# A decoder layer on one core: the last 1024 columns of the first MLP product by seven products, and the rotary queries placed elsewhere

## The chip, the cores and the metric

The kernel runs on one core of one Trainium2 chip. The metric is the time of one execution on the device in microseconds (us), smaller is better. TensorE (PE in the profile) multiplies matrices; its weight loads are shown apart as PEld. VectorE (DVE), ScalarE (ACT) and GpSimd (POOL) do the work between the products, and SyncE (SP) issues most of the DMAs. POOL and ACT issue some DMAs as well.

## The reference, cut to what matters

The program is one layer of a hybrid decoder for 512 tokens of width 1024, all in float32. Two token mixers (gated linear attention, GLA, and multi-head latent attention, MLA) work on the same normalised input, are merged by gates and projected; then comes an MLP of width 4096. Each half ends in a layer norm over a scaled residual.

```python
def reference(x, ...):
    cos, sin = rope_tables(positions)
    h = layer_norm(x, ln_in_g, ln_in_b)
    mix = token_mixer(h, cos, sin, w_in, ...)
    h = layer_norm(DEEPNORM_ALPHA * h + mix, ln1_g, ln1_b)
    ff = jnp.square(jax.nn.relu(h @ w_ff1)) @ w_ff2
    return layer_norm(DEEPNORM_ALPHA * h + ff, ln2_g, ln2_b)
```

Within the token mixer, `h @ w_in` gives, among others, 2048 columns of gate logits (1024 for each branch) and the latent queries. The queries of the eight MLA heads come out of the normalised latent queries by `w_q_b`, 128 columns a head without and 64 with a rotary embedding. In the MLP, h is 512 x 1024 and w_ff1 is 1024 x 4096.

## The kernel before, in words

**Numbers.** Each float32 operand of a product is split into a high part `hi` of a reduced format (float32r) and the remainder `lo`. A product of one block is three matmuls: hi x hi, hi x lo, lo x hi (L238 to L240 where weights are the stationary side, L271 to L273 where tokens are). Splitting a weight tile is an ACT copy (L185) and a DVE subtraction (L186).

**Weights.** All weight tiles form one list, `stream`, in the order of their use. `plan` appends entries, and `pump(i)` (L162) sees to it that entries up to i + 2 are loaded (SP DMA into `wraw`, L173) and those up to i + 1 are split (two further for entries marked `res` or `ahead`). A tile is 128 x 1024 floats. There are three buffers for `wraw` and two each for `whi` and `wlo`; a new split can start when the last matmul that read the older of the two tiles is done. Further tiles share three rings of buffers: A with 24 (`wq`, `hraw`, `hx`, `sh1`, `hid0`, `latT`, `gt`, `xh`, `xl` and others), B with 22 of half the size, and C with 8. An entry may also have a `src`, a tile that other instructions make, and a `post`, work that is done when it has been split.

**Order.** The program is written in one order, with generators (`spawn`, `tick`) that slip the side work of DVE, ACT and POOL between the matmuls. A scheduler then sets the order of the instructions on each engine before the run, by priority in the written order and by what is ready, and assigns the buffers.

**Stages around the change.** In order: input norm (`ln_transpose`, L399; it writes the transposed, normalised h, and for later also its unsplit values to DRAM as `hrawd`, L420); latents, q, k, v, r projections with GLA between them; first half of the gates (`gemm_fm`); second half of the gates by the seven-product unit (`gemm_unit("g1", ...)`, L997); `y_gla(0)`; `mla_qr(0)` (rotary queries of heads 0 to 3, L802); head pair 0; `y_gla(1)`; `mla_qr(1)`; pairs 1 to 3; output projection; norm (`h1T`, the transposed result in eight pairs of B tiles); then the MLP in four slices of 1024 hidden columns (`ci` 0 to 3). In each slice the first product with relu and square makes eight blocks of 128 hidden columns (`hid`), and the second product adds them up. Slices 0 to 2 use seven products in the second product (`win_f2`, L1257, fourteen steps `n` in the list WIN). Slice 3 uses plain products in both.

**The seven-product scheme.** A product of 2 x 2 blocks is made from seven block products instead of eight, after sums of operand blocks. In the unit the left side is four blocks of the weights, the right side four blocks of h: token halves (256 columns) by even and odd inner blocks. The list FMO (L307) gives the seven: 11, 21, t1, 22, t2, t3, t4. 11, 21, 22 are loaded blocks, t1 to t4 sums of blocks. `u_load` (L990) loads t1 and t3 as one block by SP and adds a second by an accumulating POOL DMA (L995); t2 and t4 come from t1 by DVE additions (`u_sum`, L324), as `post` of 22 and of t2. The sums of h are made by `op_sums` (L964): four sums on DVE for each of four pairs of blocks, then a split; it reads the unsplit h back from DRAM (L970). After each product partial sums are copied and added (`e1`, `e5`, `u2`, L1028 to L1041) and a quarter of the result is handed to `evac`, which for the gates is a tanh (L1054). A tile of the unit holds two inner blocks and four feature blocks, two tiles for each product; its matmuls (L1021 to L1023) have 256 columns.

**The slice to be replaced.** Slice 3 makes eight blocks in two passes of four, each 96 matmuls of 512 columns. ACT makes relu and its square as `hid0` (L1301, L1315), POOL squares again in full precision (L1316), DVE takes the remainder (L1317). The second product of the slice (`f2last`) then works through tokens 0 to 255 first, then 256 to 383, then the rest.

**Rotary queries.** `mla_qr(g)` multiplies the latent queries `qlT` (three inner blocks, two weight tiles of 512 and 256 values a lane) into 36 matmuls of 256 columns, rotates the result on DVE (L487 to L489), splits it (L114, L115) and transposes it (L821) into `QS`, which the heads read. `qlT` and the latent keys `ckT` wait in DRAM since the latents stage; `after` (L1072) loads the five tiles back (L1080).

Of the kernel before, what the change touches and what calls it, by code (L numbers as in the profile page):

```python
# [19 lines left out]
P = 128  # L20
# [32 lines left out]
def tile_hybrid_block(ctx: ExitStack, tc: tile.TileContext, I, out, dbg=None):  # L53
# [254 lines left out]
    UNITS = {"g1": ("w_in", C_G + D)}  # L308
# [13 lines left out]
    def u_sum(key, a, to, hf, x):  # L322
        t = WQ[key, (to, hf)] = WQ[key, (a, hf)]
        vtt(t, t, x, op=ALU.add)  # L324


    for key in UNITS:
        PL[key] = []
        for op, _ in FMO:
            for hf in range(2):  # L330
                PL[key].append(len(stream))
                e = {"nk": 2, "n": T, "res": False}
                if op[0] != "t":
                    e["dmas"] = [(slice(0, 2), u_src(key, int(op[0]) - 1, int(op[1]) - 1, hf), None)]
                else:
                    e["src"] = lambda q=(key, (op, hf)): WQ[q]
                if op == "22":
                    e["post"] = lambda raw, q=(key, "t1", "t2", hf): u_sum(*q, raw)
                elif op == "t2":
                    e["post"] = lambda raw, q=(key, "t2", "t4", hf): u_sum(*q, WQ[key, ("21", q[3])])  # L340
                stream.append(e)
    PL["yg", 0] = plan("w_o_gla", 0, T)
    plan_qr(0)
# [6 lines left out]
    plan_pair(0)  # L350
    PL["yg", 1] = plan("w_o_gla", T, T)
    plan_qr(1)
# [17 lines left out]
    F1 = [((0, 4), (4, 2), (6, 2))] + [tuple((b, 2) for b in range(0, 8, 2))] * 2 + [((0, 4), (4, 4))]  # L370
# [28 lines left out]
    def ln_transpose(rows, g, b, outs, hf, alt=False, n="h0"):  # L399
        tk = slice(hf * 256, (hf + 1) * 256)  # L400
        for k in range(NK):
            if len(outs) <= k:
                outs.append(A([P, 2, T], F32R, n) if n == "h0" else (B([P, T], F32R, n), B([P, T], F32R, n)))
            p = MM() if alt and k in (4, 5) else PX()
            for i in range(2):
                nc.tensor.transpose(p[:, i * P:(i + 1) * P], rows[2 * hf + i][:, k * P:(k + 1) * P], ident)
            tmp = B([P, 256], F32, "lnt")
            hi, lo = part(outs[k], 0, tk), part(outs[k], 1, tk)
            ha = act(hi, p[:, :256], AF.Identity, scale=g[:, k:k + 1], bias=b[:, k:k + 1])
            if alt and k % 2:  # L410
                act(tmp, p[:, :256], AF.Identity, scale=g[:, k:k + 1], bias=b[:, k:k + 1])
            else:
                vts(tmp, p[:, :256], g[:, k:k + 1], b[:, k:k + 1], op0=ALU.mult, op1=ALU.add)
# [10 lines left out]
    hT, rawd = [], []  # L424
# [539 lines left out]
    def op_sums(srcs, rest, new, ops):  # L964
        raws = []
# [24 lines left out]
    def u_load(key, op):  # L990
        for hf in range(2):
            t = WQ[key, (op, hf)] = A([P, 2, T], F32, "wq")
            nc.sync.dma_start(t, u_src(key, *{"21": (1, 0)}.get(op, (0, 1)), hf))
            if op != "21":
                nc.gpsimd.dma_start(t, u_src(key, *{"t1": (0, 0), "t3": (1, 1)}[op], hf), accum_op=ALU.add)  # L995

    def gemm_unit(key, ops, evac, after=None):  # L997

        bank, e1, e5, u2 = {}, {}, {}, {}
        nk = 2  # L1000
        for n, (op, ph) in enumerate(FMO):
            items = PL[key][2 * n:2 * n + 2]
            for g in range(2):
                bk = ("a" if ph in (0, 3, 6, 4) else "b", g)
                opens = ph in (0, 2, 1)
                if opens:
                    bank[bk] = (PX if ph == 1 else MM)()
                o = bank[bk]
                for hf, it in enumerate(items):
                    pump(it)  # L1010
                    hi, lo = stream[it]["w"]
                    for pp in range(nk):
                        while len(ops) <= nk * hf + pp:
                            tick(3)
                        xh, xl = ops[nk * hf + pp][ph]
                        for a in range(2):
                            c = slice((2 * g + a) * P, (2 * g + a + 1) * P)
                            oa = o[:, a * 256:(a + 1) * 256]
                            first = opens and hf == 0 and pp == 0 and a == 0
                            last = hf == 4 // nk - 1 and pp == nk - 1  # L1020
                            mm(oa, hi[:, pp, c], xh, start=first, stop=False, skip_group_check=True)  # L1021
                            mm(oa, hi[:, pp, c], xl, start=False, stop=False, skip_group_check=True)  # L1022
                            mm(oa, lo[:, pp, c], xh, start=False, stop=last, skip_group_check=True)  # L1023
                        if pp % 2:
                            tick(3)
# [3 lines left out]
                elif ph == 1:  # L1029
                    vtt(e1[g], o, e1[g], op=ALU.add)  # L1030
                    evac(0, 0, g, e1[g], None)
# [3 lines left out]
                elif ph == 3:  # L1035
# [3 lines left out]
                    evac(1, 0, g, u2[g], None)  # L1039
                elif ph == 6:  # L1040
                    vtt(e5[g], e5[g], o, op=ALU.subtract)  # L1041
                    evac(1, 1, g, e5[g], None)
                elif ph == 4:
                    evac(0, 1, g, o, None)
            if after:
                after(op)

# [14 lines left out]
    def h_sums():  # L1062
        yield from op_sums(hT, rawd,
# [8 lines left out]
    def after(op):  # L1072
# [3 lines left out]
        if op == "t4":  # L1076
            for outs, rest in ((qlT, qld), (ckT, ckd)):
# [179 lines left out]
    def win_f2(ci, hid):  # L1257
        bank = {}
        for n, (op, hf, ph) in enumerate(WIN):
# [28 lines left out]
            if n == 9 and ci + 1 < FC - 1:  # L1288
                win_load(ci + 1)

    WT = {}
    for ci in range(FC):
# [6 lines left out]
        def ev_h(a, ps):  # L1299
            r = B([P, T], F32, "relu")  # L1300
            act(r, ps, AF.Relu)  # L1301
            if win:
                if a % 2 == 0:
                    hid.append({"R": A([P, 2, T], F32, "hr")})
                ops = hid[-1]
                R = ops["R"]
                act(R[:, a % 2, :], r, AF.Square)
                if a % 2:
                    h1 = A([P, 2, 2, 256], F32R, "h1p")
                    split(R[:, :, :256], h1[:, 0], h1[:, 1])  # L1310
                    ops[0], ops[1] = [(h1[:, 0, i], h1[:, 1, i]) for i in range(2)]
                    spawn(win_hid(R, ops))
                return
            hh = A([P, 2, T], F32R, "hid0")
            act(hh[:, 0, :], r, AF.Square)  # L1315
            gtt(r, r, r, op=ALU.mult)  # L1316
            vtt(hh[:, 1, :], r, f(hh[:, 0, :]), op=ALU.subtract)  # L1317
            hid.append(hh)
# [15 lines left out]
        else:  # L1334
            bg, bb = bcast_row("ln2_g"), bcast_row("ln2_b")
            gemm_tm(PL["f2last"], hid, T, ev_res, tts=(0, 1))
# [67 lines left out]
```

## Time and profile before

| | us |
|---|---|
| runs before (3): median, lowest, highest | 903.59, 901.25, 905.59 |
| the profiled execution: its time | 902.01 |
| its span in the trace | 900.2 |
| first matmul of the gates' unit to the first of y_gla(0) | 275.21 to 317.31 |
| mla_qr(0), first to last matmul | 339.09 to 343.29 |
| last step list of win_f2 (slice 2) | 767.0 to 804.9 |
| first product of slice 3 | 805.1 to 848.4 |
| second product of slice 3 begins | 848.6 |
| last matmul starts | 892.3 |

The span runs from the first to the last instruction of the program; the execution's time is 1.8 us more. The granted clock of TensorE was 0.998 over the span. In rows of the timeline a line gives start, duration, engine, line of the source, operation, output and input tiles, and shape; an idle time in brackets comes before the instruction, with what ended it. Matmuls are pipelined, so that the next starts before the last one's duration is over; what one costs is the distance of two starts.

### The profile page before, as it was taken

The page shows a single profiled execution, that of the slowest core. Times are in us where ns is not written, and L with a number is a line of the kernel's source. Part 1 is how long each engine was busy: PE and PEld are TensorE (multiplying, and loading weights), DVE is VectorE, ACT ScalarE, POOL GpSimd, SP SyncE. Part 2 cuts the span into 40 slices and gives each one's busy share as a digit, 9 for nine tenths or more (in the row PEclk, how much of TensorE's full clock was granted, in tenths as well). Part 3 has the DMA queues.
Part 4 walks back from the last instruction along what each step waited for, and adds up shares of the span by engine and source line. Part 5 has one row for each costly group of instructions (what it writes and reads, how often), then busy time and mean ns, then how long its engine had stood idle before and what let it go on. Part 6 is the DMA issues. An engine that isn't in the chain of part 4 may idle for free.

```text
span 900.2 us, 12222 instructions
## 1 busy us (share of the span) xinstructions
PE 880.5 (98%) x4652; PEld 755.2 (84%) x4652; DVE 580.5 (64%) x945; ACT 426.9 (47%) x729; POOL 181.1 (20%) x212
## 2 busy tenths in 40 slices
PE   5999999999999999999999999999999999999996
PEld 5988888888889988888888888988888888888885
DVE  7834855577956626576856797997557646723565
ACT  5556443444546524446644423366367546733410
POOL 3203442443511001010000002104400520142200
PEclk9999999999999999999999999999999999999999
DMA  7614423217326624112207618005941990494421
GB/s 260 198 47 156 129 67 94 71 47 215 113 71 211 188 59 126 27 54 65 82 24 271 197 47 304 1 0 151 296 115 32 260 246 24 116 204 110 132 67 74
DMA packets 66699, 111.47 MB, mean 124 GB/s; under 512 B 8225, under 2 KB 28065, under 8 KB 66641
## 3 DMA queue, kind: packets, MB, share of 16 engines
q1 hardware_dynamic: 52496, 77.67, 27.5%
q0 software_dynamic: 12224, 29.37, 13.7%
q10 hardware_dynamic: 1920, 3.66, 1.2%
q8 instruction: 36, 0.59, 0.3%
q14 instruction: 23, 0.18, 0.1%
HBM read 91.28 MB, written 6.82 MB: 109 GB/s over the span
## 4 chain that ended last, share of the span: by engine, by line
PE 95%; DVE 2%; DMA 2%; ACT 1%; issue 0%; SPq 0%; DVEq 0%; POOL 0%; ACTq 0%
PE mm L238 14%; PE mm L239 14%; PE mm L240 14%; PE mm L271 7%; PE mm L273 7%; PE mm L272 7%; PE px L1275 2%; PE px L1274 2%; PE px L1273 2%; PE px L727 2%; PE mm L1275 2%; PE mm L1274 2%; PE mm L1273 2%; PE mm L1023 1%; PE mm L1021 1%; PE mm L1022 1%
## 5 line engine op out<-in xcount | busy, mean ns | idle before, releaser
L186 DVE TENSOR_TENSOR wlo<-wraw,whi 128x1024 fp32r<-128x1024 f32 (+1 forms) x102 | 115.5, 1133 | 145.1 <-ACT whi L185 141.0
L185 ACT ACTIVATE whi<-wraw 128x1024 fp32r<-128x1024 f32 (+1 forms) x102 | 98.2, 963 | 123.0 <-PE mm L239 68.3
L238 PE MATMUL mm<-h,whi 128*128 128x512 f32 x352 | 137.4, 391 | 0.0
L239 PE MATMUL mm<-h,whi 128*128 128x512 f32 x352 | 137.2, 390 | 0.0
L240 PE MATMUL mm<-h,wlo 128*128 128x512 f32 x352 | 131.3, 390 | 0.0
L1287 POOL DMA_DIRECT2D res<-ev x48 | 41.7, 1006 | 189.0 <-ACT ev L1285 153.5
L238 PEld LDWEIGHTS mm<-h,whi 128*128 128x128 f32 x352 | 66.1, 188 | 13.6 <-ACT gt L1054 0.2
L239 PEld LDWEIGHTS mm<-h,whi 128*128 128x128 f32 x352 | 66.1, 188 | 13.4
L240 PEld LDWEIGHTS mm<-h,wlo 128*128 128x128 f32 x352 | 66.0, 188 | 13.4
L272 PE MATMUL mm<-wlo,h 128*128 128x512 f32 x128 | 50.3, 393 | 0.0
L273 PE MATMUL mm<-whi,h 128*128 128x512 f32 x128 | 50.1, 392 | 0.0
L271 PE MATMUL mm<-whi,h 128*128 128x512 f32 x128 | 49.7, 403 | 0.0
L185 ACT ACTIVATE xh<-wraw 128x1024 fp32r<-128x1024 f32 (+1 forms) x28 | 27.2, 985 | 39.1 <-PE mm L273 15.8
L666 POOL TENSOR_TENSOR rp<-rp 128x256 f32<-128x256 f32 x32 | 30.3, 946 | 64.2 <-ACT E L671 47.2
L1301 ACT ACTIVATE relu<-mm 128x512 f32<-128x512 f32 x32 | 18.8, 595 | 49.5 <-PE mm L240 49.3
L186 DVE TENSOR_TENSOR wlo<-wq,whi 128x1024 fp32r<-128x1024 f32 x20 | 24.5, 1224 | 24.9 <-ACT whi L185 24.9
L186 DVE TENSOR_TENSOR xl<-wraw,xh 128x1024 fp32r<-128x1024 f32 (+1 forms) x28 | 31.2, 1128 | 10.8 <-ACT xh L185 10.8
L673 DVE TENSOR_TENSOR M<-E,qk 128x512 f32<-128x512 f32 x32 | 27.3, 854 | 14.9 <-ACT E L671 14.9
L391 POOL TENSOR_TENSOR mv<-mv,mhalf 128x1 f32<-128x1 f32 x4 | 4.6, 1156 | 146.7 <-DVE mv L390 146.7
L671 ACT ACTIVATE E<-rp 128x512 f32<-128x512 f32 x32 | 20.4, 637 | 25.6 <-POOL rp L667 25.6
L667 POOL TENSOR_TENSOR rp<-rp 128x256 f32<-128x256 f32 x32 | 28.8, 900 | 7.9 <-ACT q L696 5.7
L273 PEld LDWEIGHTS mm<-whi,h 128*128 128x128 f32 x128 | 24.0, 188 | 5.0
(405 smaller groups left out, 2412.1 us busy)
## 6 DMA issues: line engine op xcount, KB each, us to landing
wraw<-in_w_ff_dram SPq DMA_DIRECT2D x40, 512.0 KB, 4.9
wraw<-in_w_in_dram SPq DMA_DIRECT2D x38, 512.0 KB, 3.6
wq<-in_w_ff_dram POOLq DMA_DIRECT2D x24, 512.0 KB, 8.9
res<-ev POOLq DMA_DIRECT2D x48, 256.0 KB, 6.7
wraw<-in_w_o_gla_dram SPq DMA_DIRECT2D x8, 512.0 KB, 4.0
wraw<-in_w_o_mla_dram SPq DMA_DIRECT2D x8, 512.0 KB, 3.6
wraw<-in_w_out_dram SPq DMA_DIRECT2D x8, 512.0 KB, 4.2
wq<-in_w_in_dram SPq DMA_DIRECT2D x6, 512.0 KB, 5.8
```

The lines of the kernel that those rows point to most:

```text
L185: st["ins"] = act(hi[:, :nk, :n], raw[:, :nk, :n], AF.Copy)
L186: vtt(lo[:, :nk, :n], raw[:, :nk, :n], f(hi[:, :nk, :n]), op=ALU.subtract)
L238: mm(o, hi[:, c], xh, start=first, stop=False)
L239: mm(o, hi[:, c], xl, start=False, stop=False)
L240: mm(o, lo[:, c], xh, start=False, stop=last)
L271: mm(o, xh, hi[:, :n], start=opens, stop=False, skip_group_check=share)
L272: mm(o, xh, lo[:, :n], start=False, stop=False, skip_group_check=share)
L273: mm(o, xl, hi[:, :n], start=False, stop=last, skip_group_check=share)
L1273: mm(o, xh[:, c], hi[:, pp], start=opens, stop=False, skip_group_check=True)
L1274: mm(o, xh[:, c], lo[:, pp], start=False, stop=False, skip_group_check=True)
L1275: mm(o, xl[:, c], hi[:, pp], start=False, stop=hf == 1 and pp == 1, skip_group_check=True)
L1287: nc.gpsimd.dma_start(res[tt + t][:, j * T:(j + 1) * T], e, accum_op=ALU.add)
```

## The change

Three things are done.

1. The first product of slice 3 goes through the same unit as the second half of the gates. `F1` has no plain passes for it any more, and a second unit `f1` stands in the stream. Its sums of h (`h1_sums`) are started behind step 8 of the last `win_f2`, its first weight sums (t1) are loaded behind step 11, t3 and a second copy of 21 behind the unit's first product. `ev_u` makes relu, square and remainder for the quarter that the unit hands over, with the second squaring on DVE and not on POOL; quarters of the second half of the tokens are held back by four more turns of the side work. `Halves` lets `f2last` read tokens from the two halves.
2. A tile of the unit (for both uses) holds all four inner blocks and two feature blocks, 256 columns, where it held two inner blocks and four feature blocks. One tile then serves 24 matmuls in a row, and a quarter of the result is done with it. `op_sums` adds up hi and lo of h on DVE; the stores of the unsplit h to DRAM and the loads back are gone.
3. `mla_qr(0)` stands before `y_gla(0)`, and `mla_qr(1)` before `y_gla(1)`, in the program and in the stream of weights. The latent queries are loaded back behind product t2 of the gates' unit, the latent keys behind t4 as before.

The diff, cut to its core:

```diff
-    UNITS = {"g1": ("w_in", C_G + D)}
+    UNITS = {"g1": ("w_in", C_G + D), "f1": ("w_ff1", 3 * D)}
...
-    def u_src(key, i, j, hf):
+    def u_src(key, i, j, g):
         name, c0 = UNITS[key]
         src = I[name].rearrange("(k p) n -> p k n", p=P)
-        return src[:, 4 * hf + i:4 * hf + i + 3:2, c0 + j * T:c0 + (j + 1) * T]
+        c0 += j * T + g * 256
+        return src[:, i:8:2, c0:c0 + 256]
...
-                e = {"nk": 2, "n": T, "res": False}
+                e = {"nk": 4, "n": 256, "res": False}
...
+    plan_unit("g1")
+    plan_qr(0)
     PL["yg", 0] = plan("w_o_gla", 0, T)
-    plan_qr(0)
...
     plan_pair(0)
+    plan_qr(1)
     PL["yg", 1] = plan("w_o_gla", T, T)
-    plan_qr(1)
...
-    F1 = [((0, 4), (4, 2), (6, 2))] + [tuple((b, 2) for b in range(0, 8, 2))] * 2 + [((0, 4), (4, 4))]
+    F1 = [((0, 4), (4, 2), (6, 2))] + [tuple((b, 2) for b in range(0, 8, 2))] * 2 + [()]
...
         else:
+            plan_unit("f1")
             plan_zip("f2last", [("w_ff2", 0, fb, True), ("w_ff2", T, fb, True)])
...
-            else:
-                if len(rawd) <= k:
-                    rawd.append(DR([P, T], "hrawd"))
-                nc.gpsimd.dma_start(rawd[k][:, tk], tmp)
...
-            while len(raws) < min(4, p + 2):
-                raws.append(A([P, 2, T], F32, "hraw"))
-                for i in range(2):
-                    nc.sync.dma_start(raws[-1][:, i], rest[2 * len(raws) - 2 + i])
-            raw = raws[p]
+            raw = A([P, 2, T], F32, "hraw")
+            for i in range(2):
+                h = srcs[2 * p + i]
+                vtt(raw[:, i], f(part(h, 0, slice(0, T))), f(part(h, 1, slice(0, T))), op=ALU.add)
+            yield
...
+        def prod(op):
+            ph = dict(FMO)[op]
+            opens = ph in (0, 2, 1)
             for g in range(2):
...
+                o, it = bank[bk], PL[key, op, g]
+                pump(it)
+                hi, lo = stream[it]["w"]
+                for k in range(4):
+                    while len(ops) <= k:
+                        tick(3)
+                    xh, xl = ops[k][ph]
+                    for a in range(2):
+                        c = slice(a * P, (a + 1) * P)
+                        oa = o[:, a * 256:(a + 1) * 256]
+                        mm(oa, hi[:, k, c], xh, start=opens and k == 0 and a == 0, stop=False, skip_group_check=True)
+                        mm(oa, hi[:, k, c], xl, start=False, stop=False, skip_group_check=True)
+                        mm(oa, lo[:, k, c], xh, start=False, stop=k == 3, skip_group_check=True)
+                    if k % 2:
+                        tick(3)
...
-        if op == "t4":
-            for outs, rest in ((qlT, qld), (ckT, ckd)):
+        if op in ("t2", "t4"):
+            for outs, rest in {"t2": ((qlT, qld),), "t4": ((ckT, ckd),)}[op]:
...
+    mla_qr(0)
     WID[0] = 2
     y_gla(0)
-    mla_qr(0)
...
     mv()
+    mla_qr(1)
     y_gla(1)
-    mla_qr(1)
...
+            if ci == FC - 2 and n == U0:
+                t_h1.append(spawn(h1_sums()))
+            if ci == FC - 2 and n == U1:
+                u_load("f1", "t1")
...
+    U0, U1 = 8, 11
...
+            def ev_u(j, i, g, ps, sb):
+                def later():
+                    for _ in range(1 + 4 * i):
+                        yield
+                    r = ps if sb else B([P, T], F32, "relu")
+                    act(r, ps, AF.Relu)
+                    hh = A([P, 2, 2, 256], F32R, "hid0")
+                    act(hh[:, 0], r.rearrange("p (a c) -> p a c", a=2), AF.Square)
+                    yield
+                    vtt(r, r, r, op=ALU.mult)
+                    vtt(hh[:, 1], r.rearrange("p (a c) -> p a c", a=2), f(hh[:, 0]), op=ALU.subtract)
+                    hts[j, i, g] = hh
+                spawn(later())
...
+            gemm_unit("f1", hops, ev_u, after1)
+            hid = [Halves(hts, j, g, a) for j in range(2) for g in range(2) for a in range(2)]
             gemm_tm(PL["f2last"], hid, T, ev_res, tts=(0, 1))
```

More of the change, by code (lines that the diff above doesn't have):

```diff
@@ L1006, in gemm_unit @@
                 if opens:
[L1007 to L1025, printed above, removed]
+                    bank[bk] = (PX if ph == 1 else (pb or MM) if ph == 2 else MM)()
@@ L1062, in h_sums @@
     def h_sums():
-        yield from op_sums(hT, rawd,
+        yield from op_sums(hT,
                            lambda: [[B([P, 2, 256], F32R, "sh") for _ in range(2)] for _ in range(2)], hops)
@@ L1289, in win_f2, with __init__, __getitem__, h1_new @@
                 win_load(ci + 1)
+            if ci == FC - 2 and n == U0:
+                t_h1.append(spawn(h1_sums()))
+            if ci == FC - 2 and n == U1:
+                u_load("f1", "t1")
+    class Halves:
+        def __init__(self, ts, j, g, a):
+            self.ts, self.j, self.g, self.a = ts, j, g, a
+        def __getitem__(self, ix):
+            _, w, c = ix
+            i, t0 = divmod(c.start, 256)
+            while (self.j, i, self.g) not in self.ts:
+                tick(4)
+            return self.ts[self.j, i, self.g][:, w, self.a, t0:t0 + P]
+    hops, t_h1 = [], []
+    def h1_new():
+        t = [A([P, 2, 2, 256], F32R, "sh1") for _ in range(2)]
+        return [(x[:, 0], x[:, 1]) for x in t]
+    def h1_sums():
+        yield from op_sums(h1T, h1_new, hops)
     WT = {}
+    U0, U1 = 8, 11
     for ci in range(FC):
@@ L1301, in ev_h @@
             act(r, ps, AF.Relu)
[L1302 to L1318, printed above, removed]
+            if a % 2 == 0:
+                hid.append({"R": A([P, 2, T], F32, "hr")})
+            ops = hid[-1]
+            R = ops["R"]
+            act(R[:, a % 2, :], r, AF.Square)
+            if a % 2:
+                h1 = A([P, 2, 2, 256], F32R, "h1p")
+                split(R[:, :, :256], h1[:, 0], h1[:, 1])
+                ops[0], ops[1] = [(h1[:, 0, i], h1[:, 1, i]) for i in range(2)]
+                spawn(win_hid(R, ops))
         for b, w in F1[ci]:
```

58 lines of the change are left out of this document (31 added, 27 removed).

## The prediction

> **What bounds the kernel now.** I read the page first, for the engine that ends last.
>
> ```profile
> span 900.2 us, 12222 instructions
> ...
> PE 880.5 (98%) x4652; PEld 755.2 (84%) x4652; DVE 580.5 (64%) x945; ACT 426.9 (47%) x729; POOL 181.1 (20%) x212
> ...
> PE 95%; DVE 2%; DMA 2%; ACT 1%; issue 0%; SPq 0%; DVEq 0%; POOL 0%; ACTq 0%
> ```
>
> TensorE (PE) is busy 98% and is 95% of the chain that ended last. A change pays only by taking matmul time away, or a wait of PE. How much waiting there is to take, the waits of PE say (total, times, longest, in us):
>
> ```profile
> PE px L406 <- ACT x L395: 9.1, 1, 9.1
> PE px L860 <- DVE PT L112: 0.7, 1, 0.7
> PE mm L238 <- DVE qn L115: 0.6, 1, 0.6
> PE px L406 <- DVE lnt L413: 0.5, 1, 0.5
> PE mm L1023 <- DVE wlo L186: 0.5, 1, 0.5
> ```
>
> The 9.1 us are the start, before any product. What is left is some 3 us in the whole run, and no wait lies in the last slice of the first MLP product. Two stages are to be compared: the one that is replaced, and the one that already works by seven products (L1021 to L1023). Windows: length, busy time of each engine, clock, DMA share, GB/s.
>
> ```profile
> 275.20:317.30 42.10, 41.62 (x345) 41.31 (x344) 28.36 (x30) 25.72 (x38) 3.32 (x3) 1.00 0.65 201
> 767.00:805.00 38.00, 38.00 (x169) 31.48 (x168) 22.38 (x23) 23.44 (x33) 10.36 (x12) 1.00 0.74 162
> 805.10:848.60 43.50, 43.50 (x193) 36.05 (x192) 14.65 (x12) 14.96 (x22) 8.74 (x8) 1.00 0.51 137
> ```
>
> The first is the seven-product unit of the gates, the second the last windowed part of the second MLP product, the third the slice to be replaced: 192 matmuls in 43.5 us, VectorE (DVE, third busy time) only 14.7 us busy. Matmuls overlap, so a price is start to start, not duration. Their starts, from the timeline:
>
> ```profile
> 805.10 0.39 PE L238 MATMUL mm<-h,whi 128*128 128x512 f32 x1
> 805.33 0.39 PE L239 MATMUL mm<-h,whi 128*128 128x512 f32 x1
> ...
> 310.81 0.28 PE L1021 MATMUL mm<-h,whi 128*128 128x256 f32 x1
> 310.93 0.28 PE L1022 MATMUL mm<-h,whi 128*128 128x256 f32 x1
> 311.69 0.39 PE L1023 MATMUL mm<-h,wlo 128*128 128x256 f32 x1 [0.48 <-DVE wlo L186]
> ```
>
> 512 columns cost 43.5/192 = 0.2267 us, 256 columns 0.120 us, so halves cost 6% more per column. The last line is the one wait inside the old unit: 0.76 us start to start, 0.64 over the pitch.
>
> **The change, part by part**
>
> *1. Matmuls.* Removed: 192 at 0.2267 = 43.5 us. Added: 7 products x 4 pairs of inner blocks x 4 feature blocks x 3 = 336 of 256 columns, at 0.120 = 40.3 us. **-3.2 us.** The old unit confirms it: 42.1 us less 0.9 of transposes (L790) in it less the 0.64 wait is 40.6. So 7/8 of the work comes out as 0.93 of the time. In that row the weight loads (second busy time) fill 41.3 of 42.1 us, against 36.1 of 43.5 in the slice: each weight load serves half as many columns. The Trainium skill, "Perfetto Trace Analysis" (Identifying the Most-Contended Engine), judges TensorE's headroom by weight-load busy share, and by it the seven products run into the loads; the row agrees.
>
> *2. Waits in the new unit.* One tile is now used by 24 matmuls in a row, 24 x 0.120 = 2.88 us. In that time the next must be split, in the slot that just came free (two each of whi, wlo): ACT 1.06 (L185) then DVE 1.22 (L186) = 2.28. Slack 0.6, less semaphores. DVE's load in 40.3 us: 14 splits x 1.22 = 17.1; 4 tile sums x 1.22 (L324) = 4.9; 6 partial sums x 0.68 (L1030, L1038, L1041) = 4.1; squares and remainders 16 x 0.68 = 10.9, half of which may lie under the next product, which first reads the first half of the tokens. That is 31.6 us, 78%, against 67% in the old unit. The square leaves POOL: L1317 took 1.52 beside L1316's POOL work and 0.68 without, so DVE pays no more per block than before. The old unit lost 0.64 at such collisions. Bounds: 0 (all fit) and 4 us (a collision of 0.3 in each of 14 tiles). I take +0.6, the row of the same shape.
>
> *3. Operands of the unit.* op_sums on h1T: per pair of blocks 2 adds x 0.68, 4 sums x 0.41, 2 remainders x 0.68; times four, 17.4 us of DVE. It starts at product 8 of 14 of the window stage, where DVE is idle 15.6 of 38.0 us, and is due at the third product, 11.5 us into the unit. DVE idles there too: 0. The weight sum t1: one SP load (L993, median 5.8 us), then an accumulating POOL load (L995, 10.4), 16.2 us. Its split must begin by 805.1 + 3 x 2.88 = 813.7, so its loads by 797.5. They are written behind product 11, which ends at 767.0 + 12 x 2.72 = 799.6, 2.1 too late; but SP runs ahead of what is written: w_o_gla's first tile, written some 6 us before its use at 317, was issued at 284. On POOL the result additions (L1287) stand behind the accumulating load; nobody reads res before 868. DMA: 16 loads of 512 KB for 8, +4.2 MB on some 12 MB in 82 us, about 200 GB/s, as in the old unit's window. Taken 0; bounds 0 and +8 (a rival).
>
> *4. The old unit.* Its tiles hold two feature blocks, so each evacuation comes 2.88 us after the last, not 1.44: four gate activations (L1054) no longer stand ahead of one split, which made the 0.64 wait; behind it PE itself is next. **-0.3**, between -0.64 and +1. Its operands are added up on DVE (8 x 0.68 = 5.4 us) where they were read back from DRAM. Around 215 to 257 us DVE is busy 36.7 of 42.0, so this just fills it; but 257 to 275 has 13 us free, and the sums are due at 287. Taken 0; bounds 0 and +2. 16 POOL stores (L420, 0.54 each) and 8 SP loads (L970) go; PE's waits at the start are on DVE, not on these: 0, at best -0.7.
>
> *5. Rotary queries.* mla_qr(0) (36 matmuls, 6 small DMAs for both groups, 2.3 us each) moves from behind y_gla(0) to before it. Gone: the wait L238 <- DVE qn, 0.76 over the pitch, where DVE had the rotations (L487 to L489) among the splits of the first head pair. New: its last weight tile is used by 12 matmuls, 1.44 us, and behind it now comes a w_o_gla tile, whose split takes 2.28 + 0.15. PE waits 1.0, with all its later matmuls behind, while ACT and DVE run on; before, a small tile followed (0.63 + 0.69 = 1.32, hidden). Also y_gla takes four accumulators, two of which the rotations still hold (4 x 0.74 us of DVE): +0.3. The three latT loads pass w_o_gla's on SP; already now all five land by 311, and 317 is early enough. mla_qr(1) moves likewise, but attention heads fill PE there: 0. **Net +0.5**, between -0.8 and +2.
>
> **Sum:** -3.2 + 0.6 - 0.3 + 0.5 = **-2.4 us**. On the profiled execution: 902.0 (span 900.2) to 899.6. That execution lies inside the three runs, 1.6 below their median of 903.6; the same step from the median gives **901.2 us**.
>
> By the Trainium skill, "TensorE: Matmul & The Clock Gate" (Wait — 56ns, not 53.3ns?), a warm matmul costs N/2.4 GHz + 2.5 ns, 215.8 and 109.2 ns: 41.4 to 36.7 us, -4.7 for part 1 and 899.7 in all. The rows say 226.7 and 120, and are used.
>
> **Rivals**
>
> - *Every cover holds* (chance 0.14): no wait in the unit, those of the old unit and of qn gone, 0.7 off the start: -3.2 - 0.64 - 0.76 - 0.7 = -5.3, **898.3 us**. For it: PE has almost no waits now, the order of instructions being planned ahead. Against it: the 2.28 in 2.88 us, and the 1.44 us tile before y_gla.
> - *Halves cost half* (0.03): 256 columns at 0.2267/2, 336 x 0.1134 = 38.1, 2.2 less: **899.0 us**. Against it: 336 such matmuls at 0.120. The skill's formula above points this way.
> - *t1 comes late* (0.18): its two tiles and ten of op_sums share a ring of 24 with the eight operand tiles of the window stage, freed only by its last two products. If t1's first load starts x us after 797.5, PE stands x us before the third product. If it must wait for the end of the window stage, 804.9, x is 7.4: -2.4 + 7.4 = +5.0, **908.6 us, slower**. It decides from 804.4 on (x = 6.9, that is +4.5). For it: the ring is shared by all stages. Against it: by product 8, I count 15 of the 24 in use.
> - *DVE collides at each tile* (0.14): 14 x 0.3 = 4.2 in place of 0.6: **904.8 us**, and no change to be told.
> - *My sum* (0.51).
>
> A measurement of this kernel can tell about 0.5%, 4.5 us: faster is below 899.1, slower above 908.1. Nearly all of *every cover holds*, half of *halves cost half* and a little of my sum is faster: 0.16. Slower, *t1 late* at its far end, or with collisions on top: 0.19. Within: 0.65. The range 897.8 to 908.0 reaches from just past the best case to near the worst and leaves out what lies beyond.
>
> **What would show it.** Right: 336 matmuls of 256 columns behind the window stage at 0.120 us, the stage 40.5 to 41.5 us long; a wait of about 1 us at y_gla's first matmul behind qr; no wait on qn L115. Wrong: a PE wait on DVE wlo L186 whose source is wq, with the POOL load landing just before it (t1 late); many short waits on L186 in the unit (collisions); waits in 215 to 290 us, where the added adds displace the gated attention's levels.

## The result, and the profile after

| | before | after |
|---|---|---|
| runs, us: median (lowest to highest) | 902.14 (901.25 to 905.59), 11 runs | 908.79 (905.66 to 911.93), 11 runs |
| ratio, 95% interval | | 1.0064 [1.0048, 1.0079] |
| span of the profiled run, us | 900.2 | 908.8 |
| slice 3: first product begins | 805.10 | 803.68 |
| slice 3: second product begins | 848.6 | 854.1 |
| slice 3's first matmul to the end of the span | 95.13 | 105.08 |

The changed kernel is slower by 0.64%. It lies 0.8 us above the range and 7.6 above the forecast. As a step the miss is larger: 2.4 us less were forecast from a median of 903.59, and the medians above differ by 6.65 us the other way. The profile was taken of an execution of 910.53 us, 1.7 above its median, so what follows accounts for the 8.5 us between the two spans. The page of the changed kernel:

```profile
span 908.8 us, 12549 instructions
...
PE 882.4 (97%) x4796; PEld 762.7 (84%) x4796; DVE 617.0 (68%) x1009; ACT 439.7 (48%) x749; POOL 173.1 (19%) x192
...
PE 90%; DMA 5%; DVE 3%; ACT 1%; issue 1%; DVEq 0%; ACTq 0%; POOLq 0%
```

TensorE's share of the chain that ended last went from 95% to 90%, and that of DMA from 2% to 5%. The table says where: up to slice 3 the changed kernel is 1.4 us ahead, and from there on it loses 9.9. The whole stage in one line (length, then busy time of PE, weight loads, VectorE, ScalarE and POOL, then granted clock, DMA share, GB/s; its first 0.28 us still belong to the window's last two matmuls, the unit's first starts at 803.68):

```profile
803.40:854.10 50.70, 42.24 (x314) 40.74 (x314) 34.81 (x45) 26.50 (x37) 8.29 (x8) 0.93 0.78 179
```

Of the 336 matmuls, 24 run on among the second product's, so 312 at 0.120 = 37.4 us of work fill the 50.4 us from 803.68 on: 13.0 are lost. The waits of TensorE in that stretch (total, times, longest):

```profile
PE mm L1018 <- DVE wlo L186: 2.7, 2, 1.6
PE mm L1016 <- ACT e L1029: 2.6, 1, 2.6
PE px L1016 <- ACT whi L185: 1.6, 1, 1.6
PE px L1018 <- DVE wlo L186: 1.5, 2, 0.8
```

Counted start to start, less the pitch, they are 1.21 at 806.7, 0.22 and 0.92 around 811, then 1.75 and 0.92 at 815 to 818, and 2.77 and 1.80 at 831 to 836: 9.6 us in all. The names at the right are DVE and ACT, which looks like a collision on the splits. ScalarE's own rows say otherwise. In the last bracket of a row stand its idle time and what ended it:

```profile
815.59 1.06 ACT L185 ACTIVATE whi<-wraw 128x1024 fp32r<-128x1024 f32 x1 [3.69 <-DMA wraw<-in_w_ff_dram]
832.00 1.06 ACT L185 ACTIVATE whi<-wraw 128x1024 fp32r<-128x1024 f32 x1 [4.79 <-DMA wraw<-in_w_ff_dram]
832.97 0.58 ACT L1029 ACTIVATE e<-mm 128x512 f32<-128x512 f32 x1
```

Before both long waits ScalarE itself stood 3.7 and 4.8 us, for a weight tile. The first is the second tile of product 21 (issued 803.44, landed 815.48), the second is that of product 22 (issued 821.57, landed 831.90). The copy `e` that the wait at 831 is put down to ran that late because it stood behind that tile's split in ScalarE's order. So 7.2 of the 9.6 us start from plain weight loads that landed late. A tile of the same 512 KB with the machine quiet, at 853.94, landed in 3.5 us; here it took 10 to 13.

The other 2.4 us, at 806 to 812, can be followed back to an earlier row of ScalarE:

```profile
792.65 0.60 ACT L1286 ACTIVATE ev<-mm 128x512 f32<-128x512 f32 x1 [6.24 <-DMA res<-ev]
```

It stood 6.2 us for an evacuation buffer that an addition to the residual still held; that addition was issued at 784.33 and landed at 792.54. The first copies of the sums of h stand behind it in ScalarE's order, and the last sum was split only at 812.1, among the unit's first tiles.

The five-us slices show where the DMA engines are full. The last two numbers are DMA share and GB/s; the times of packets overlap, so a share can pass 1. Before:

```profile
810.00:815.00 5.00, 5.00 (x24) 4.14 (x23) 1.23 (x1) 1.06 (x1) 0.01 (x1) 1.00 1.04 179
815.00:820.00 5.00, 5.00 (x24) 4.14 (x23) 1.23 (x1) 1.06 (x1) 0.00 (x0) 1.00 0.33 99
```

After:

```profile
805.00:810.00 5.00, 3.95 (x33) 3.75 (x32) 4.67 (x10) 3.00 (x6) 3.44 (x5) 1.00 1.17 225
810.00:815.00 5.00, 4.19 (x32) 3.68 (x30) 2.50 (x3) 1.90 (x3) 0.66 (x1) 1.00 1.15 214
815.00:820.00 5.00, 2.65 (x13) 2.34 (x13) 3.10 (x4) 3.75 (x5) 0.00 (x0) 0.81 1.12 233
...
830.00:835.00 5.00, 1.49 (x11) 1.08 (x9) 2.97 (x4) 2.49 (x3) 0.00 (x0) 1.00 1.17 252
835.00:840.00 5.00, 4.26 (x25) 4.27 (x26) 3.05 (x3) 0.21 (x1) 0.00 (x0) 0.66 0.71 168
```

Before, the share is near 1 until 815 and falls to a third when the window's residual additions are through. After, it is 1.05 or more from 795 to 835. What fills it is in the queues' view of 795 to 835 (packets, MB, share of 16 engines; q0 holds the accumulating DMAs of POOL, q1 the plain ones of SP), first before:

```profile
q0 software_dynamic: 1395, 2.53, 37.0%
q1 hardware_dynamic: 1632, 3.15, 26.0%
```

then after:

```profile
q0 software_dynamic: 3370, 4.66, 70.2%
q1 hardware_dynamic: 4751, 5.21, 41.4%
```

In 40 us, 70.2% for 4.66 MB is 6.0 us of all 16 engines per MB; 41.4% for 5.21 MB is 3.2. A megabyte that is accumulated costs about twice a plain one, and the shares add up to 112%. SP adds to it: it issues in order, and the four loads of t3 and of the second 21 were written ahead of 22's second tile.

```profile
803.44 4.90 SPq L173 DMA_DIRECT2D wraw<-in_w_ff_dram  x2
808.44 13.04 SPq L991 DMA_DIRECT2D wq<-in_w_ff_dram  x4
821.57 6.29 SPq L173 DMA_DIRECT2D wraw<-in_w_ff_dram  x3
```

The issues at 803.44 and 807.98 took 0.37 us each; the four behind them took 1.9 to 5.5 and held SP's queue for 13 us, though their data is needed last. The tile that TensorE waited for at 831 was issued only after them.

Last, the clock. Two slices show 0.81 and 0.66. Matmuls on both sides of the end of the first slow stretch (start, duration):

```profile
821.22 0.41 PE L1018 MATMUL px<-h,wlo 128*128 128x256 f32 x1
...
821.71 0.28 PE L1018 MATMUL px<-h,wlo 128*128 128x256 f32 x1
821.83 0.28 PE L1016 MATMUL px<-h,whi 128*128 128x256 f32 x1
```

One takes 0.41 us, the next ones 0.28; start to start it is 0.2135 us in the slow stretch, and 0.120 behind it. The records give a granted clock of 0.5 for 818.1 to 821.5 and for 835.2 to 838.6, 3.413 us each, and each follows on a stretch of that length in which TensorE mostly stood. Start to start, less the pitch, the first cost 1.6 us (17 matmuls) and the second 1.3 (13). Five more times the first matmul behind a wait took 0.22 to 0.23 us, 0.5 lost in all. Waits 9.6, clock 2.9 and these 0.5 make the 13.0. The Trainium skill, "TensorE: Matmul & The Clock Gate" (What's actually happening), says that the clock falls to half after at least one idle window of about 3.4 us. The trace agrees on the length and on the half; but the two windows here weren't wholly idle, as a few matmuls ran in each.

### The profile page after: what moved, and what is told of

The parts are those of the page before. It is cut to its first block, busy times and chain, and to the rows that moved or that the text cites. A ratio compares the mean times of both kernels' runs of the same rounds, so it can differ in the third digit from the quotient of the medians.

```text
span 908.8 us, 12549 instructions
## 1 busy us (share of the span) xinstructions
PE 882.4 (97%) x4796; PEld 762.7 (84%) x4796; DVE 617.0 (68%) x1009; ACT 439.7 (48%) x749; POOL 173.1 (19%) x192
## 4 chain that ended last, share of the span: by engine, by line
PE 90%; DMA 5%; DVE 3%; ACT 1%; issue 1%; DVEq 0%; ACTq 0%; POOLq 0%
PE mm L238 12%; PE mm L240 12%; PE mm L239 12%; PE mm L271 7%; PE mm L273 7%; PE mm L272 7%; DMA wraw<-in_w_ff_dram 3%; PE mm L1018 2%; PE mm L1017 2%; PE mm L1016 2%; PE px L1275 2%; PE px L1274 2%; PE px L1276 2%; PE px L726 2%; DMA res<-ev 2%; PE mm L1276 1%
## 5 line engine op out<-in xcount | busy, mean ns | idle before, releaser
L186 DVE TENSOR_TENSOR wlo<-wraw,whi 128x1024 fp32r<-128x1024 f32 (+1 forms) x100 | 112.8, 1129 | 114.2 <-ACT whi L185 106.3
L238 PE MATMUL mm<-h,whi 128*128 128x512 f32 x288 | 112.7, 392 | 0.0
L239 PE MATMUL mm<-h,whi 128*128 128x512 f32 x288 | 112.4, 390 | 0.0
L240 PE MATMUL mm<-h,wlo 128*128 128x512 f32 x288 | 107.1, 390 | 0.0
L239 PEld LDWEIGHTS mm<-h,whi 128*128 128x128 f32 x288 | 54.1, 188 | 10.9
L238 PEld LDWEIGHTS mm<-h,whi 128*128 128x128 f32 x288 | 54.0, 188 | 11.0
L240 PEld LDWEIGHTS mm<-h,wlo 128*128 128x128 f32 x288 | 53.9, 188 | 11.0
L186 DVE TENSOR_TENSOR wlo<-wq,whi 128x1024 fp32r<-128x1024 f32 x28 | 34.3, 1224 | 22.0 <-ACT whi L185 21.9
L665 POOL TENSOR_TENSOR rp<-rp 128x256 f32<-128x256 f32 x32 | 31.6, 988 | 61.2 <-ACT E L670 44.8
L185 ACT ACTIVATE whi<-wq 128x1024 fp32r<-128x1024 f32 x28 | 29.6, 1056 | 20.7 <-PE mm L1017 15.8
L1016 PE MATMUL mm<-sh,whi 128*128 128x256 f32 x128 | 36.8, 288 | 2.6 <-ACT e L1029 2.6
L1018 PE MATMUL mm<-sh,wlo 128*128 128x256 f32 x128 | 37.0, 289 | 1.6 <-DVE wlo L186 1.6
L1017 PE MATMUL mm<-sh,whi 128*128 128x256 f32 x128 | 36.7, 287 | 0.0
L186 DVE TENSOR_TENSOR xl<-wraw,xh 128x1024 fp32r<-128x1024 f32 (+1 forms) x28 | 31.3, 1130 | 5.3 <-ACT xh L185 5.3
```

The lines of the kernel that those rows point to most:

```text
L185: st["ins"] = act(hi[:, :nk, :n], raw[:, :nk, :n], AF.Copy)
L186: vtt(lo[:, :nk, :n], raw[:, :nk, :n], f(hi[:, :nk, :n]), op=ALU.subtract)
L238: mm(o, hi[:, c], xh, start=first, stop=False)
L239: mm(o, hi[:, c], xl, start=False, stop=False)
L240: mm(o, lo[:, c], xh, start=False, stop=last)
L1016: mm(oa, hi[:, k, c], xh, start=opens and k == 0 and a == 0, stop=False, skip_group_check=True)
```

## The experiments

The theory: **the DMA engines are full from 795 to 835**, by the unit's 16 loads (four of them accumulating) together with the residual additions of the window stage (16 in all); tiles land late, and the clock drops after the long waits. Rivals: the loss lies in the other two parts of the change; the splits and sums on DVE collide in any case; the evacuation buffers, held by the additions, are the cause; the work is only started too late.

**1. Without the new unit** (slice 3's first product plain, the rest of the change kept).

```diff
-    F1 = [((0, 4), (4, 2), (6, 2))] + [tuple((b, 2) for b in range(0, 8, 2))] * 2 + [()]
+    F1 = [((0, 4), (4, 2), (6, 2))] + [tuple((b, 2) for b in range(0, 8, 2))] * 2 + [((0, 4), (4, 4))]
...
-            plan_unit("f1")
...
-            gemm_unit("f1", hops, ev_u, after1)
```

> The changed kernel, but slice 3 makes its first product by plain passes again, with the old relu, square and remainder. What is left of the change are the unit's tiles of two feature blocks, the sums of h on VectorE and the moved rotary queries. Theory (the loss lies in the new unit alone): the changed kernel's trace reached the slice 1.7 us earlier than the one before (803.4 against 805.1 us), and that stays: 900.4 us, 0.2% under the kernel before. Rival (the earlier arrival is borrowed and given back later, or is chance between executions): 902.1 us, as before.

Measured: 901.27 us, ratio 0.9982 [0.9971, 0.9993]; slice 3 begins at 803.51, and TensorE has no wait behind 755. The time lies between the two that were expected, 900.4 and 902.1. The other two parts gain a little, and the whole loss belongs to the unit.

**2. The late-needed loads held back** (t3 and the second 21 are issued behind 22's last tile; same bytes).

```diff
-                if op == "11":
-                    u_load("f1", "t3")
-                    u_load("f1", "21")
+                if op == "t1":
+                    with tc.issue_after(st["dmai"].ins):
+                        u_load("f1", "t3")
+                        u_load("f1", "21")
```

> The changed kernel; only the loads of t3 and of the second copy of 21 for the new unit are written behind its product t1 and held on SP until the last loaded tile of 22 has been issued. Theory A (DMA): those four loads held SP for 12.8 us (1.9, 1.9, 5.5 and 3.5 us to issue) ahead of the second tile of 22, which was issued at 821.6, and shared the DMA engines with the tiles needed next. Then the waits before 831 and 834 us (2.8 and 1.8 us) and the second stretch at half clock (1.7 us) go, perhaps half of the wait at 815 as well: 902 to 904 us. Rival B (VectorE and ScalarE collide at each tile): nothing goes, 908.8 us. Rival C: t3 is now late itself and the waits move to the sixth product: 906 us or more.

Measured: 905.73 us, ratio 1.0035 [1.0021, 1.0048]. The waits at 831 to 836 are gone, and no half clock is left; smaller ones come at 824 and 840. The second product begins at 849.2, not 854.1. The waits at 807 to 818 stay, 5.0 us, and the DMA share is still 1.09 or more from 805 to 835. SP's order was some 5 of the 13 us by the traces, 3.1 by the medians, less than was expected; the engines are as full as they were. The waits at 815 to 818 are nearly those of the changed kernel (1.72 and 0.92 here), yet no half clock follows. In both traces the changes of the granted clock lie whole multiples of 3.413 us apart. Counted so, the changed kernel's two waits fall into one such window, 814.69 to 818.10, and these into two, as one window ends at 817.77. So the length of a wait alone didn't decide.

**3. Without the residual additions of the third slice** (what its expectation says is left out).

```diff
-                        nc.gpsimd.dma_start(res[tt + t][:, j * T:(j + 1) * T], e, accum_op=ALU.add)
+                        if ci < FC - 2:
+                            nc.gpsimd.dma_start(res[tt + t][:, j * T:(j + 1) * T], e, accum_op=ALU.add)
```

> The changed kernel, but the 16 additions of the third slice's second product to the residual (POOL DMAs of 256 KB) are left out, so that this part of the result is missing. Theory A (DMA): from 795 to 835 us the DMA share was 1.05 to 1.17, and tiles took 12 to 13 us to land. Without these 4 MB of additions the tiles land in some 5 us, the waits of the unit from 814 us on (7.2 us) and most of the two half-clock stretches (3.4 us) go: 898 to 901 us. Rival B (collisions on VectorE and ScalarE): they do the same work as before, 907 us or more.

Measured: 898.25 us, ratio 0.996 [0.9947, 0.9974]. The queues from 795 to 835, and the waits of TensorE behind 790:

```profile
q1 hardware_dynamic: 4515, 5.25, 41.8%
q0 software_dynamic: 2112, 2.10, 34.2%
```

```profile
PE mm L1018 <- DVE wlo L186: 1.3, 2, 0.9
```

The same unit with the same loads: q1 is unchanged and q0 halved, 76% in place of 112%. Two waits are left, 0.57 and 1.07 us start to start, and no half clock. Ahead of the first, at 817.7, DVE works without a pause: a collision on the splits. Ahead of the second, at 824.2, ScalarE and DVE had stood 1.9 and 1.6 us for the second tile of 22, which took 12.95 us to land. So a late tile remains, and the DMA share is still 0.97 to 1.14 from 805 to 820; but 21's second tile was issued at 797.67 in place of 803.44. Even the waits at 807 to 812, which the profile puts down to DVE and ACT (21's first tile had landed at 794), are gone. With no addition to hold a buffer, the copies of the sums start on ScalarE at 787.8 (793.1 in the changed kernel) and the last sum is split at 808.5 (812.1). By these rows the chain of those 2.4 us begins at a held buffer. This run, which takes away the holding and the transfers at once, can't say whether the transfers that slow the addition itself would have to go.

**4. Earlier start** (sums of h behind step 4, t1 behind step 8).

```diff
-    U0, U1 = 8, 11
+    U0, U1 = 4, 8
```

> The changed kernel with both starting points moved four and three products ahead: the sums of h behind product 4 of the last window stage, the loads of t1 behind product 8. Theory A (DMA): the additions of t1 come before the crowded stretch, and in the planned order on SP the second tile of 22 now stands ahead of t3 and 21: the waits from 814 us on shrink by half or more, 902 to 905 us. Rival B (VectorE late with the sums, the waits at 806 to 812 us): those 2.3 us go and the rest stays, 906.5 us. Rival C: the ring of 24 is short in the window stage, and the waits move into it: 908 us or more.

Measured: 902.63 us, ratio 1.0012 [1.0003, 1.0022]. In the unit 1.9 us of waits are left, but a new one stands in the window stage: TensorE waits 3.36 us at 790.9 for an evacuation (`ev`, L1286), whose buffer a residual addition still holds, and the half clock follows at 794.5. The trace is of an execution of 905.68 us, 3.0 above the median, so the usual one may lose less there. Start time counts, but at least in this execution it moves part of the loss ahead of the unit.

**5. The sums of h alone** (the kernel before, with `op_sums` from hi and lo and no stores and loads of the unsplit h).

```diff
-                nc.gpsimd.dma_start(rawd[k][:, tk], tmp)
...
+                vtt(raw[:, i], f(part(h, 0, slice(0, T))), f(part(h, 1, slice(0, T))), op=ALU.add)
```

> The kernel before with one part of the change alone: the sums of h in the gates' unit are made from hi and lo on VectorE, and the 16 stores of the unsplit h by POOL and the 8 loads back are gone. In the changed kernel the first 192 matmuls (latents) ended 1.1 us earlier than before (46.7 against 47.8 us). Theory (the stores crowd the loads and the queues at the start): the 1.1 us come from this part, 901.0 us. Rival (the prediction: PE's waits at the start are on VectorE, not on the stores; the 1.1 us come from elsewhere): 902.0 us.

Measured: 902.23 us, ratio 0.9995 [0.9985, 1.0005]. The start ends 0.5 us earlier and a wait of 0.71 at 244.5 comes in, where DVE has the added sums. No change to be told.

**6. Rotary queries at their old places**, against experiment 1.

```diff
-    plan_qr(0)
     PL["yg", 0] = plan("w_o_gla", 0, T)
+    plan_qr(0)
...
-    mla_qr(0)
     WID[0] = 2
     y_gla(0)
+    mla_qr(0)
...
```

> e1_no_f1_unit (901.27 us) with the rotary queries at their old places and all latents loaded back behind t4: the tiles of two feature blocks and the sums on VectorE are left. Theory (the move gains the qn wait of 0.76 and, with luck, that of 0.78 before the heads at 432 us, and loses 0.68 ahead of y_gla, so 0.9): 902.1 us. Rival (the prediction: the move costs 0.5): 900.8 us.

Measured: 901.92 us, ratio 0.9994 [0.9986, 1.0003]. The waits of 0.75 at 348 and 0.78 at 431 are back and that of 0.68 at y_gla is gone. Experiment 1 has 901.27, ratio 0.9982 [0.9971, 0.9993]: by the traces the move gains 0.85 us of waits, by the medians 0.65, but the intervals of the two ratios overlap, so the gain isn't certain.

**7 and 8. One load of 21.** The unit needs this block twice, for product 21 and for the sum t4, and loads it twice. Here it is loaded once, into the ring, and kept; t3's loads are written behind product 21 and held behind 22's last tile. The starts U0, U1 are 8, 9 in 7, and 5, 7 in 8.

```diff
-                if op[0] != "t":
+                if op[0] != "t" and not (key == "f1" and op == "21"):
...
+                u_load("f1", "21")
...
-    U0, U1 = 8, 11
+    U0, U1 = 5, 7
...
-                if op == "11":
-                    u_load("f1", "t3")
-                    u_load("f1", "21")
+                if op == "21":
+                    with tc.issue_after(st["dmai"].ins):
+                        u_load("f1", "t3")
```

> The changed kernel with two loads of 512 KB fewer in the crowded stretch: block 21 of w_ff1 is loaded once, into the ring of 24, and serves as the second product's weights and in the sum t4; t3 is loaded behind product 21, on SP held behind the last tile of 22; the loads of 21 and t1 are written behind product 9 of the window stage. Theory A (DMA): 14 loads for 16, and 22 finds its buffers earlier. The waits from 814 us on (7.2 us with 3.4 us of half clock) shrink by half: 903 us. Rival C (the ring is short): 21 is late itself, a wait before the second product, 906 us or more.

> As e7_one_21, with the sums of h behind product 5 and the loads of 21 and t1 behind product 7. Theory A (DMA): the crowd is spread further, 901 to 902.5 us, about the kernel before. Rival (evacuations wait for buffers that the additions to the residual hold: with the loads earlier, those additions land later, as in e4_early, where PE waited 3.4 us in the window stage): 903 us or more.

Measured: 7 gives 901.27 us, ratio 0.9989 [0.9978, 0.9999]; 8 gives 900.45 us, ratio 0.9981 [0.9968, 0.9994]. Both are faster than was expected, and neither has a half clock in the unit; 7 still has 3.7 us of waits there. The two longest waits of 8 behind 790:

```profile
PE px L1274 <- ACT whi L185: 1.0, 1, 1.0
PE px L1275 <- DVE wlo L186: 0.5, 1, 0.5
```

They lie in the window's last steps (L1274, L1275), not among the unit's own products, where none is over 0.44. One megabyte less of loads, and the rest in the order of need and earlier, takes the loss away; which of the three did most these two runs don't separate. Kernel 8 is faster than the kernel before by 0.2%, about as much as leaving the unit out gives. But its DMA engines are hardly emptier. Its queues from 795 to 835:

```profile
q0 software_dynamic: 3692, 4.98, 72.6%
q1 hardware_dynamic: 3798, 4.52, 36.4%
```

That is 109%, where the changed kernel had 112%, and no five us of it are under 0.93. Yet 22's tiles landed within 5.3 and 7.3 us of their issue, 13.2 and 10.3 in the changed kernel. When they were issued, three and four transfers had not yet landed, and seven and six in the changed kernel. So full engines alone don't stop TensorE; what does is a tile that is asked for late and behind others while they are full.

**9 to 11. The residual additions computed, not transferred.** 9: the changed kernel with the 16 additions of the third slice on POOL; 10: half on POOL, half on DVE; 11: kernel 8 with the additions as in 10.

```diff
-                        nc.gpsimd.dma_start(res[tt + t][:, j * T:(j + 1) * T], e, accum_op=ALU.add)
+                        rr = res[tt + t][:, j * T:(j + 1) * T]
+                        if ci < FC - 2:
+                            nc.gpsimd.dma_start(rr, e, accum_op=ALU.add)
+                        else:
+                            gtt(rr, e, rr, op=ALU.add)
```

> The changed kernel, in which the 16 residual additions of the third slice's window are computed by POOL (one addition of 128x512 each) and no longer done by accumulating DMAs; all else as it was. If those transfers are what makes the unit's tiles late (DMA share 1.05 to 1.17 from 795 to 835), the tiles land in time, no half clock follows, and the time is 898.3 (as with the additions left out) plus what POOL's additions cost: two of 128x256 take 0.99 us each on POOL, so about 2 us each, 32 us in all, during which the evacuation buffers are held and DVE may run slower; 898 to 902. If the loss came from the evacuation buffers being held and not from the transfers, it stays, since POOL holds them as long: 905 to 909, waits of TensorE on weight splits after 815.

> As the kernel with POOL's additions, but the additions of every second token block are on DVE (8 x about 0.68 us) and 8 on POOL (16 us). If the transfers were the cause: 898 to 900, and no more than the kernel with all on POOL, since buffers come free sooner; DVE is full from 785 to 805, so up to 2 us may be lost at the operand sums. If the held buffers were the cause, this one is well below the kernel with all on POOL.

> The kernel with one load of 21, t3 held behind 22's tiles and the earlier start (5, 7), with the additions split between POOL and DVE. It had 2.8 us of waits left, 1.8 of them on the window's last steps. With both reliefs of the DMA: 897.5 to 899, the best so far. If the DMA was no limit any more in that kernel, it stays at 900.4 or loses up to 2 us by DVE's added work in the window stage.

Measured: 914.32 us, ratio 1.0132 [1.0117, 1.0148]; 913.54 us, 1.0124 [1.0111, 1.0138]; 904.32 us, 1.0026 [1.0017, 1.0035]. All three are slower than was expected under either theory. The stretch 785 to 825 in the changed kernel, then in 9 (third busy time DVE, fifth POOL, then clock and DMA share):

```profile
785.00:825.00 40.00, 35.70 (x202) 31.11 (x201) 31.34 (x47) 20.94 (x32) 13.30 (x15) 0.96 1.05 228
```

```profile
785.00:825.00 40.00, 29.89 (x138) 24.41 (x137) 39.56 (x41) 16.52 (x26) 25.88 (x16) 0.88 0.61 150
```

The DMA share fell from 1.05 to 0.61 as meant, but DVE is busy 39.6 of 40 us with fewer instructions. The same split of a tile (L186) at the same place, in 9 and in the changed kernel:

```profile
784.98 2.31 DVE L186 TENSOR_TENSOR xl<-T,xh 128x1024 fp32r<-128x1024 f32 x1
```

```profile
785.01 1.23 DVE L186 TENSOR_TENSOR xl<-T,xh 128x1024 fp32r<-128x1024 f32 x1 [3.33 <-ACT xh L185]
```

Beside POOL's additions, about 2.0 us each there, it takes nearly twice as long. The Trainium skill, "SBUF — State Buffer" (SBUF: two separate sides), says that DVE and GpSimd take a shared port in turns, each holding it for its whole instruction, where DVE has two inputs from SBUF; the rows agree. These runs exchange one full resource for another, and the weight loads were also issued later behind DVE (21's second tile at 807.2, not 803.4). So they don't tell held buffers from transfers, which stays open for the 2.4 us of experiment 3.

## Why the prediction was wrong, point by point

**The step that failed is the DMA price in part 3**: "+4.2 MB on some 12 MB in 82 us, about 200 GB/s, as in the old unit's window. Taken 0". It averaged over two stages and counted bytes. Both hid what mattered: half of the added bytes are accumulated, and a part of the 82 us was already full, with shares of 0.87 to 1.07 from 790 to 815 in the kernel before. That kernel's own queues had the prices: 37.0% of 40 us for 2.53 MB is 5.9 us per MB accumulated, 26.0% for 3.15 MB is 3.3 plain. With these the unit's 12 plain and 4 accumulating loads cost 6.3 x 3.3 + 2.1 x 5.9 = 33 us of all 16 engines, where the eight tiles they replace cost 4.2 x 3.3 = 14; and they start where the additions (4.2 MB, 25 us) are still running. Measured, against experiment 3: from slice 3's first matmul to the end 105.1 us with the additions and 93.9 (897.18 - 803.23) without, so 11.1 us for additions and loads together, against the 0 taken and beyond the bound of 8. (Some 2.4 of it go by the held buffer.) The bytes alone don't make the price: kernel 8 keeps the additions and all but one megabyte of the loads, and loses nothing. The order and the start of the issues belong to the step that was taken as 0.

- *Matmuls, -3.2: right.* The pitch is 0.120. In experiment 3 the stage lasts 39.3 us for 312 matmuls; less its 1.6 of waits that is 37.6, against 37.4.
- *Waits in the unit, +0.6: the mechanism right.* Experiment 3 has one such collision, 0.57; its other wait, 1.07, starts from a late tile. The 1.6 of both stand in the sum below.
- *The sums of h, 0 (part 3): right in experiment 3,* where no wait stands at 806 to 812. In the changed kernel, where the held buffer puts them off by 3.6 to 5.3 us, they cost the 2.4 us there.
- *The old unit, -0.3, and its operands, 0: nearly right.* The 0.64 wait is gone, the start is 1.1 us shorter (its 192 matmuls end at 46.7, not 47.8; the bound was 0.7), and 0.71 came in at 243.9, where the added sums displace the gated attention's work. The prediction named that place as a risk and priced it at nothing. In experiment 5, where the start gains 0.5, the two together come to nothing.
- *Rotary queries, +0.5: wrong in sign by the traces.* The new wait at y_gla is there, 0.68 where 1.0 was taken, and that on qn is gone. Not taken was that the moves remove another, 0.78 at 431, which is back when they are undone (experiment 6); it stood among the five waits shown, as PE px L860.
- *The rival "t1 comes late", 908.6:* its time is right by luck, its mechanism isn't. t1's accumulating loads landed at 808.1 and 817.1. The tiles that stopped TensorE were plain ones, 21 and 22, and not the ring but the engines and SP's order held them back.
- *Collisions at each tile:* not seen; experiment 3 has one.

The sum with measured terms: -3.2 + 1.6 + 11.1 = +9.5 from slice 3's begin on, 9.9 measured (0.4 is not accounted for), and 1.4 gained ahead of it: +8.5, the difference of the two spans.

The seven products do take TensorE time away, but no gain in the whole is shown. With the additions left out there are 3.0 us between the medians of experiments 1 and 3 (901.27 and 898.25) and 1.8 between their spans, part of which the missing additions may give. With nothing left out and the loads in order, kernel 8's median is 0.8 us under experiment 1's, but the ratios to the kernel before are the same, 0.9981 and 0.9982: the unit then costs nothing and gains nothing that can be told.

## What to carry to other kernels

Price a DMA by its kind and in the stretch where it runs: share of the 16 engines per megabyte, from the queues' view of the kernel at hand, added to the share that is already there; a mean in GB/s over a long window hid a full stretch here. A full stretch is a warning and not yet a loss: ask then which tile is needed first, when it is issued and what stands ahead of it. Loads that are needed last belong behind those needed first on the queue that issues them; here four such issues held the queue for 13 us. A scheme that saves an eighth of the matmuls but loads twice the tiles must find the DMA time for them first.

## What the runs showed of the hardware that wasn't expected

- Accumulating DMAs took 5.8 to 6.5 us of the 16 engines per MB, plain ones 3.2 to 3.3, each pair in the same 40 us (the kernel before, the changed one, experiments 3 and 8).
- A share of 112% went with 13.0 us lost on TensorE in the unit, one of 109% with no wait over 0.44 us there (kernel 8).
- An issue on SP took 0.37 us when the engines were idle, and also at 803.4 and 808.0, at shares of 1.10 and 1.17; the six behind those, to 823.0, took 1.3 to 5.5 us.
- Two waits of 1.75 and 0.92 us halved the granted clock for 3.413 us, at a cost of 1.6; waits of 1.72 and 0.92 in experiment 2 didn't. The first pair lay within one window of 3.413 us, the second across two.
- DVE's split of 128x1024 took 2.31 us beside a POOL addition and 1.23 without.
